# Retention's output product with three block pairs instead of two: their weight sums made ahead, the last head's norm inverted on 128x256, the head gates multiplied 1024 wide

## The chip, the cores and the metric

The kernel runs on one core of a Trainium2 chip. The metric is device time in microseconds of one execution, the median over the runs shown. The profile is that of one execution; its times count from its first instruction.

## What is computed

Two layers over 512 tokens and a model width of 1024, then a final RMSNorm, all in float32. Of each layer:

```python
h = rmsnorm(x, g_mix)
z = h @ w_in                      # attention q,k,v | retention q,k,v,g | gate_a | gate_b
A = sliding_window_sink_attention(...)
r = chunkwise_retention(rq, rk, rv)                       # 4 heads, 256 values each
r = r * lax.rsqrt(jnp.mean(r * r, axis=-1, keepdims=True) + EPS)
r = r.reshape(B, S, 1024) * jax.nn.silu(rg)
mixed = sigmoid(ga) * (A @ w_a) + sigmoid(gb) * (r @ w_b)
x = x + mixed @ w_out
x = x + jnp.square(jax.nn.relu(rmsnorm(x, g_mlp) @ w_up)) @ w_down
```

The change lies in r's norm and gate and in r @ w_b. The sizes are w_b and w_out 1024x1024, w_in 1024x5888, w_up 1024x4096.

## The kernel before, in words

**Tiles and passes.** Activations are held with features on the 128 partitions and the 512 tokens along the free axis, in eight tiles per 1024 features. Float32 products go through TensorE (PE) as float32r in three passes: each operand is split into a high half and the rest, and hi x hi, hi x lo and lo x hi are summed in PSUM (`products`, L332 to L334).

**Weight units.** All weights come in units of 128x1024 in one fixed list (`unit_order`). A unit is loaded into a raw tile (`load_until`, L196), then ScalarE (ACT) copies it to the high half (L286) and VectorE (DVE) subtracts that from the raw tile to give the low half (L287). The pool `wpool` has three buffers each for raw, hi and lo; `unit()` asks for units up to two ahead of the one that PE takes. In the rows, raw_N, hi_N and lo_N are these tiles.

**Chunks and pairs.** A plain chunk (`chunk`) makes one tile of 128 output features from one unit: 8 contraction tiles by 3 passes, 24 matmuls of 512 columns. `narrow_pair` makes two output tiles at once by Strassen's scheme: the weights and the input are cut in 2x2 blocks (tokens in halves of 256, called H), and 7 block products of 4 contraction tiles by 3 passes are done, 84 matmuls of 256 columns. It takes four units, called parts: parts 0, 1 and 2 hold two block products each, part 3 one. Some blocks are sums of weights, some inputs are sums of activations. What it needs:

- Sums of activations, made once for a product: `sum_input` for each half of it, four wide additions on lines 626, 627, 629 and 630, then splits into float32r halves (ACT L339, DVE L340). Their tiles in the rows are sums_N; the halves go to the slots r0 to r13.
- Sums of weights. Either `add_part` makes them on DVE when the part is split (L252 for part 0, L255 for part 1, L259 and L260 for part 2, into raw3_N), or, for the pairs that `PARKED` lists, `ahead()` makes them earlier in the layer: it loads both units (`raws_ahead`, L234), does four DVE additions (`sums_ahead`, L241 to L246) and stores the sums in DRAM; the parts are then loaded from there in 256 KB pieces (`load_part`, L219). Each call of `ahead()` finishes one set and starts the loads of another. Calls stand between the two chunks of qk(1), in values(0), and after units 0, 1 and 3 of w_a.

**Order of the stages in a layer.** w_in in groups and chunks with attention running as `background` steps between them; w_a; the rest of w_in, again with retention's heads as background steps; then `mixed_pair(0)` and `mixed_pair(2)` over w_b (each pair's output is multiplied by its gate on L1244 and added to the attention part on L1247), `sum_input` for the first half of w_out's input, then the four plain chunks of w_b (output multiplied on L1218 and added on L1219), `sum_input` for the second half, and w_out: two output tiles by `two_chunks` (put into x on L1288) and three pairs (c = 2, 4, 6; only the last is parked; put into x on L1296). The tiles of x are loaded back for w_out by eight loads (L1278), the gates for w_b by loads of gate_N (L1203). What comes of w_b is split into float32r halves (`split_mixed`, L339 and L340), for the pairs in steps delayed into the next pair.

**Last head.** `Head.norm` gives the inverse root mean square, on 128x512 for the last head (`inverse_rms`: ACT root, DVE reciprocal on L480). `Head.finish` multiplies each of the head's two output tiles by it (L1089), then by the gate (L1090).

**What sets the order.** The code's order, the pools and a scheduler that the framework runs when the kernel is built set the order of instructions on each engine; at run time each engine and each DMA queue goes strictly in order. All loads and stores named here are issued from SP's queue. An instruction that waits for its operands holds all behind it.

## Time and profile before

| what | before |
|---|---|
| median of 3 runs | 1468.94 us |
| lowest and highest | 1468.91 and 1469.76 us |
| span of the profiled execution | 1467.5 us, clock 1.000 |
| ACT busy | 814.6 us, 1306 instructions |
| DMA | 198.65 MB, mean 135 GB/s |

The runs give no other time for the profiled execution than its span, from the first instruction to the last; the runs' times take in what lies around it. A row of the profile reads: line, engine, operation, output from inputs by the program's names without numbers, count, busy time, mean ns of one, and the idle time ahead of it with its releaser. PE is TensorE's matmuls, PEld its weight loads.

The stages of layer 0 by the clock of this execution (length; busy time and count of PE, PEld, DVE, ACT, POOL; granted clock; DMA share; GB/s): from 285 retention's second half ends under the last chunks of w_in, from 318.7 the two w_b pairs run, from 343.3 w_b's last chunks and w_out's first two tiles, and from 368.7 the w_out pairs begin.

```profile
285.00:318.70 33.70, 33.70 (x152) 27.89 (x151) 28.27 (x35) 20.02 (x25) 0.00 (x0) 1.00 0.44 140
318.70:343.30 24.60, 24.60 (x190) 23.68 (x189) 16.26 (x22) 11.14 (x17) 0.00 (x0) 1.00 0.75 241
343.30:368.70 25.40, 25.40 (x115) 21.03 (x114) 25.14 (x34) 13.09 (x16) 0.00 (x0) 1.00 0.62 200
368.70:402.00 33.30, 33.21 (x260) 31.95 (x259) 30.16 (x46) 20.92 (x34) 0.00 (x0) 1.00 0.39 118
```

The second layer has the same stages 728 us later.

### The profile page before, as it was taken

How to read it: one execution, taken by the hardware profiler on the slowest of the kernel's cores; microseconds unless marked ns; L12 is line 12 of the kernel's file. 1: busy time of each engine (PE TensorE's matmuls, PEld its weight loads, DVE VectorE, ACT ScalarE, POOL GpSimd, SP SyncE). 2: the span in 40 equal slices, each digit the busy share in tenths (PEclk: the TensorE clock that was granted, in tenths of full speed). 3: DMA queues.
4: the chain of work that ended last, by engine and by line, in shares of the span. 5: the costliest groups of instructions: out<-in, count | busy, mean ns of one | idle time of the engine just before them, and what ended most of it. 6: DMA issues, size and time to landing. Idle time of an engine off the chain costs nothing.

```text
span 1467.5 us, 20166 instructions
## 1 busy us (share of the span) xinstructions
PE 1461.0 (100%) x7434; PEld 1246.4 (85%) x7434; DVE 1161.6 (79%) x1912; ACT 814.6 (56%) x1306; POOL 3.7 (0%) x14
## 2 busy tenths in 40 slices
PE   9999999999999999999999999999999999999998
PEld 7888888888988888888888888888989888888887
DVE  7998778678988787776678977786899877877774
ACT  7657356654684445444456653666547754455544
POOL 0000000000000000000000000000000000000000
PEclk9999999999999999999999999999999999999999
DMA  6423843356443332333543258323654432333373
GB/s 227 134 87 101 280 166 98 104 171 210 130 120 125 101 115 88 107 108 115 165 121 102 86 168 285 107 95 107 191 197 123 144 101 87 125 105 101 108 200 108
DMA packets 73346, 198.65 MB, mean 135 GB/s; under 512 B 8712, under 2 KB 8864, under 8 KB 73248
## 3 DMA queue, kind: packets, MB, share of 16 engines
q1 hardware_dynamic: 72960, 196.84, 42.5%
q8 instruction: 58, 0.95, 0.3%
q10 hardware_dynamic: 288, 0.52, 0.1%
q14 instruction: 40, 0.33, 0.1%
HBM read 173.73 MB, written 20.98 MB: 133 GB/s over the span
## 4 chain that ended last, share of the span: by engine, by line
PE 99%; DVE 0%; issue 0%; POOLq 0%; ACT 0%; DVEq 0%; ACTq 0%
PE mm L334 24%; PE mm L332 23%; PE mm L333 23%; PE mm L1356 11%; PE mm L1357 6%; PE rv L332 2%; PE rv L334 2%; PE rv L333 2%; PE score L864 1%; PE r L332 1%; PE r L334 1%; PE r L333 1%; PE pT L819 0%; PE pv L846 0%; PE pv L845 0%; PE warm L311 0%
## 5 line engine op out<-in xcount | busy, mean ns | idle before, releaser
L333 PE MATMUL mm<-r,hi 128*128 128x512 f32 (+1 forms) x1568 | 572.5, 367 | 0.0
L332 PE MATMUL mm<-r,hi 128*128 128x512 f32 (+1 forms) x1568 | 569.9, 367 | 0.0
L334 PE MATMUL mm<-r,lo 128*128 128x512 f32 (+1 forms) x1568 | 563.9, 367 | 0.2
L286 ACT ACTIVATE hi<-raw 128x1024 fp32r<-128x1024 f32 (+1 forms) x334 | 333.9, 1002 | 377.8 <-PE mm L333 206.9
L287 DVE TENSOR_TENSOR lo<-raw,hi 128x512 fp32r<-128x512 f32 (+1 forms) x335 | 384.3, 1150 | 110.8 <-ACT hi L286 109.4
L334 PEld LDWEIGHTS mm<-r,lo 128*128 128x128 f32 x1568 | 293.6, 188 | 48.8 <-DVE lo L287 1.4
L332 PEld LDWEIGHTS mm<-r,hi 128*128 128x128 f32 x1568 | 294.1, 188 | 46.5 <-ACT r L342 0.2
L333 PEld LDWEIGHTS mm<-r,hi 128*128 128x128 f32 x1568 | 294.3, 188 | 46.0
L1356 PE MATMUL mm<-r,hi 128*128 128x512 f32 x728 | 252.0, 391 | 0.0
L1357 PE MATMUL mm<-r,lo 128*128 128x256 f32 x728 | 200.3, 277 | 0.0
L1356 PEld LDWEIGHTS mm<-r,hi 128*128 128x128 f32 x728 | 136.5, 188 | 28.7 <-ACT mm L1383 0.2
L1357 PEld LDWEIGHTS mm<-r,lo 128*128 128x128 f32 x728 | 136.7, 188 | 3.2 <-DVE lo L287 0.6
L1429 ACT ACTIVATE z<-z 128x512 f32<-128x512 f32 x56 | 32.5, 624 | 51.8 <-DVE z L1409 51.8
L1436 DVE TENSOR_TENSOR x<-x,mm 128x512 f32<-128x512 f32 x56 | 37.7, 686 | 28.1 <-PE mm L334 28.1
L334 PE MATMUL rv<-hi,r 128*128 128x512 f32 x128 | 49.8, 389 | 0.0
L333 PE MATMUL rv<-lo,r 128*128 128x512 f32 x128 | 49.8, 389 | 0.0
L332 PE MATMUL rv<-hi,r 128*128 128x512 f32 x128 | 49.8, 390 | 0.0
L339 ACT ACTIVATE r<-z 128x512 fp32r<-128x512 f32 x64 | 38.5, 619 | 16.3 <-DVE z L1090 16.1
L340 DVE TENSOR_TENSOR r<-z,r 128x512 fp32r<-128x512 f32 x64 | 42.9, 685 | 4.7 <-ACT r L339 4.3
L891 ACT ACTIVATE sm<-sm,st 128x256 f32<-128x256 f32 (+1 forms) x64 | 30.1, 472 | 19.0 <-DVE st L879 18.8
L1409 DVE SCALAR_TENSOR_TENSOR z<-z,rstd 128x512 f32<-128x512 f32 x52 | 35.6, 685 | 0.6
L340 DVE TENSOR_TENSOR r<-sums,r 128x1024 fp32r<-128x1024 f32 x24 | 28.9, 1216 | 0.0
(270 smaller groups left out, 1679.2 us busy)
## 6 DMA issues: line engine op xcount, KB each, us to landing
raw<-w_in_in SPq DMA_DIRECT2D x89, 512.0 KB, 3.6
raw<-w_down_in SPq DMA_DIRECT2D x64, 512.0 KB, 3.6
raw<-w_up_in SPq DMA_DIRECT2D x32, 512.0 KB, 3.9
raw<-w_up_in SPq DMA_DIRECT2D x60, 256.0 KB, 2.9
raw<-w_a_in SPq DMA_DIRECT2D x8, 512.0 KB, 6.5
ahead<-w_b_in SPq DMA_DIRECT2D x8, 512.0 KB, 5.4
park_w_b<-ahead SPq DMA_DIRECT2D x16, 256.0 KB, 5.9
ahead<-w_up_in SPq DMA_DIRECT2D x8, 512.0 KB, 5.7
```

The costliest lines, as they stand in the source:

```text
L286: nc.scalar.activation(hi[:, at], raw[:, at], AF.Copy)
L287: last_low[:] = [nc.vector.tensor_tensor(lo[:, at], raw[:, at], f32(hi[:, at]), ALU.subtract).ins]
L332: nc.tensor.matmul(ps, ah, bh, start=start and i == 0, stop=False, **more)
L333: nc.tensor.matmul(ps, ah, bl, start=False, stop=False, **more)
L334: nc.tensor.matmul(ps, al, bh, start=False, stop=stop and i == n - 1, **more)
L339: nc.scalar.activation(hi, src, AF.Copy)
L340: nc.vector.tensor_tensor(lo, src, f32(hi), ALU.subtract)
L1356: nc.tensor.matmul(both, hi[:, c], m, start=start and k == 0, stop=False, **more)
L1357: nc.tensor.matmul(ps[:, :H], lo[:, c], m[:, 0, :], start=False, stop=k == 3 and start, **more)
L1409: nc.vector.scalar_tensor_tensor(z[:, :, at], z[:, :, at], 0.0, factor, ALU.max, ALU.mult)
L1429: nc.scalar.activation(z[:, i, :], z[:, i, :], AF.Square)
L1436: nc.vector.tensor_tensor(x[:, c, :], x[:, c, :], ps, ALU.add)
```

## The change

In each layer chunks 4 and 5 of w_b become a third `mixed_pair(4)`, and its weight sums are parked like those of the first two. `ahead()` is called once more, between the two chunks of qk(2). The last head's norm uses `inverse_rms_halved`: two roots on 64x256, a reciprocal on 128x256 (L469), and four copies that spread it to 128x512 (L472). `Head.finish` multiplies both output tiles of a head by the norm, and by the gate, in one instruction of 1024 columns each. The pairs of w_b take their PSUM banks from ps_mm only for c = 2, from ps_aux for c = 0 and 4 (before: ps_aux for 0, ps_mm for 2). The weights are packed on the host accordingly.

```diff
@@ -51,7 +51,7 @@
 ASIDE = 48
 FIRST_WIDE, LAST_WIDE = 6, 32
 BETWEEN = (0, 2, 4, 5)
-PARKED = (("w_b", 0), ("w_b", 2), ("w_out", 6), ("w_up", 4), ("w_up", 6))
+PARKED = (("w_b", 0), ("w_b", 2), ("w_b", 4), ("w_out", 6), ("w_up", 4), ("w_up", 6))
 H = T // 2
 CROSSED = (0, 1, 4, 5, 2, 3, 6, 7)
 
@@ -65,7 +65,7 @@
         return [("pair", j, part, src) for j in firsts for part in range(4)]
 
     order = plain("w_in", 26) + plain("w_a", 4) + plain("w_in", 26, 46)
-    order += pairs("w_b", 0, 2) + plain("w_b", 4, 8)
+    order += pairs("w_b", 0, 2, 4) + plain("w_b", 6, 8)
     order += plain("w_out", 2) + pairs("w_out", 2, 4, 6)
     for what, q, i in mlp_sequence():
         if what == "first":
@@ -1080,16 +1080,16 @@
 
             def norm(self):
                 self.inv = temp("inv")
-                (inverse_rms if self.h == 3 else inverse_rms_apart)(self.parts, RET_V, self.inv)
+                (inverse_rms_halved if self.h == 3 else inverse_rms_apart)(self.parts, RET_V, self.inv)
 
             def finish(self):
                 h = self.h
+                two = rg_tiles[h]
+                nc.vector.tensor_tensor(two, two, self.inv.unsqueeze(1).broadcast_to([P, 2, T]), ALU.mult)
+                nc.vector.tensor_tensor(two, self.both, two, ALU.mult)
                 for e in range(2):
-                    z = rg.pop(2 * h + e)
-                    nc.vector.tensor_tensor(z, z, self.inv, ALU.mult)
-                    nc.vector.tensor_tensor(z, self.rr[e], z, ALU.mult)
                     hi, lo = slots.one(), slots.one()
-                    split(view(hi), view(lo), z)
+                    split(view(hi), view(lo), rg.pop(2 * h + e))
                     ret[2 * h + e] = (hi, lo)
 
         def retention(pair):
@@ -1173,7 +1173,7 @@
             slots.give(*t[1])
 
         background.append(retention(0))
-        qk(2)
+        qk(2, between=ahead)
         qk(3)
         values(1)
         drain()
@@ -1243,7 +1243,7 @@
             def put(i, at, src, z):
                 return nc.vector.tensor_tensor(two[:, i, at], two[:, i, at], src, ALU.mult)
 
-            narrow_pair(ps_aux if c == 0 else ps_mm, delayed_step(), form_of(by_form_r), block_r, put)
+            narrow_pair(ps_mm if c == 2 else ps_aux, delayed_step(), form_of(by_form_r), block_r, put)
             nc.vector.tensor_tensor(two, two, x[:, own : own + 2, :], ALU.add)
             delayed.extend(partial(split_mixed, c + i, gates[c + i]) for i in range(2))
 
@@ -1251,7 +1251,7 @@
             at = slice(tokens * H, tokens * H + H)
             return [tuple(m[:, at] for m in rT[CROSSED[k]]) for k in range(4 * half, 4 * half + 4)]
 
-        for c in (0, 2):
+        for c in (0, 2, 4):
             mixed_pair(c)
         all_of(delayed)
         delayed.clear()
@@ -1260,7 +1260,7 @@
         homes_m = [forms_home(), None, forms_home(), None]
         by_form_m = [h and h[1] for h in homes_m]
         sum_input(by_form_m, gate_tiles[:2], 0)
-        for c in range(4, KD):
+        for c in range(6, KD):
             if c % 2 == 0:
                 gate_tile()
             chunk("w_b", layer, rT, put_mixed(c))
@@ -1559,8 +1559,8 @@
 
 def _ret_units(w):
     cols = _crossed(np.arange(D))
-    paired = _units_chunks(w[cols], cols[:T])
-    return [_swapped(u) if i % 2 else u for i, u in enumerate(paired)] + _units_chunks(w, cols[T:])
+    paired = _units_chunks(w[cols], cols[: 6 * P])
+    return [_swapped(u) if i % 2 else u for i, u in enumerate(paired)] + _units_chunks(w, cols[6 * P :])
 
 
 def _up_units(w):
```

DVE, last head of retention, layer 0, before (z_2514 holds the head's two gates, rr_2496 its outputs, inv_2628 the norm, lo_2758 and lo_2793 are weight units, sums_2695 is `sum_input`'s):

```order
L340 TENSOR_TENSOR r11_87<-z_2349,r11_87 128x512
L287 TENSOR_TENSOR lo_2758<-raw_2668,hi_2757 128x1024
L480 RECIPROCAL inv_2628<-inv_2628 128x512
L287 TENSOR_TENSOR lo_2793<-raw_2720,hi_2792 128x1024
L1089 TENSOR_TENSOR z_2514<-z_2514,inv_2628 128x512 x2
L1090 TENSOR_TENSOR z_2514<-rr_2496,z_2514 128x512 x2
L627 TENSOR_TENSOR sums_2695<-z_2514,sums_2695 128x512
```

The same place after (z_2524, rr_2506, own_2641 with inv_2638, lo_2770 and lo_2805, sums_2707):

```order
L287 TENSOR_TENSOR lo_2770<-raw_2682,hi_2769 128x1024
L469 RECIPROCAL own_2641<-own_2641 128x256
L287 TENSOR_TENSOR lo_2805<-raw_2732,hi_2804 128x1024
L1088 TENSOR_TENSOR z_2524<-z_2524,inv_2638 128x1024
L1089 TENSOR_TENSOR z_2524<-rr_2506,z_2524 128x1024
L627 TENSOR_TENSOR sums_2707<-z_2524,sums_2707 128x512
```

The reciprocal has half the columns and stands between the same two weight splits; four multiplications of 512 have become two of 1024.

DVE, from the last w_b pair's end, before (gate_3020 is the second pair's output, gate_3162 and gate_3234 are those of the plain chunks, mm_N their PSUM banks):

```order
L287 TENSOR_TENSOR lo_3167<-raw_3093,hi_3166 128x1024
L627 TENSOR_TENSOR sums_3152<-gate_3020,sums_3152 128x512
L629 TENSOR_TENSOR sums_3153<-gate_3020,gate_2893 128x512
L287 TENSOR_TENSOR lo_3202<-raw_3127,hi_3201 128x1024
L340 TENSOR_TENSOR r1_77<-gate_3020,r1_77 128x512 x2
L630 TENSOR_TENSOR sums_3153<-gate_3020,sums_3152 128x512
L340 TENSOR_TENSOR r7_83<-sums_3152,r7_83 128x4x256
L1218 TENSOR_TENSOR gate_3162<-mm_3170,gate_3162 128x512
L1218 TENSOR_TENSOR gate_3162<-mm_3205,gate_3162 128x512
L287 TENSOR_TENSOR lo_3241<-raw_3164,hi_3240 128x1024
```

After, from the same point of the third pair (gate_3163 is its output, gate_3032 and gate_2905 are those of the first two, gate_3305 that of the two chunks left, lo_3273 the split of chunk 7's unit, lo_3312 and lo_3347 those of w_out's first two units):

```order
L287 TENSOR_TENSOR lo_3273<-raw_3202,hi_3272 128x1024
L627 TENSOR_TENSOR sums_3295<-gate_3032,sums_3295 128x512
L630 TENSOR_TENSOR sums_3296<-gate_3032,sums_3295 128x512
L340 TENSOR_TENSOR r7_83<-sums_3295,r7_83 128x4x256
L1244 TENSOR_TENSOR gate_3163<-gate_3163,mm_3165 128x256
L1218 TENSOR_TENSOR gate_3305<-mm_3315,gate_3305 128x512
L340 TENSOR_TENSOR r10_86<-sums_3296,r10_86 128x4x256
L1247 TENSOR_TENSOR gate_3163<-gate_3163,x_75 128x1024
L287 TENSOR_TENSOR lo_3312<-raw_3236,hi_3311 128x1024
L1219 TENSOR_TENSOR gate_3305<-gate_3305,x_75 128x512
L287 TENSOR_TENSOR lo_3347<-raw_3270,hi_3346 128x1024
```

Before, the splits of two chunks (lo_3167, lo_3202) and `sum_input`'s additions lie between the last pair and the split of w_out's first unit (lo_3241). Now chunk 7's split and the second half of those additions stand ahead of the last pair's L1247, and w_out's first unit (lo_3312) right behind it.

DVE, from the third part of w_out's first pair (lo_3401 before, lo_3472 after) to the next pair's first split (lo_3468 before, lo_3539 after); L343 and L429 prepare the MLP's input, L678 and L675 are additions of the pair that read PSUM:

```order
L287 TENSOR_TENSOR lo_3401<-raw3_3397,hi_3400 128x1024
L255 TENSOR_TENSOR raw2_3430<-raw_3393 128x512
L287 TENSOR_TENSOR lo_3433<-raw_3238,hi_3432 128x512
L1296 TENSOR_TENSOR x_75<-x_75,mm_3389 128x256
L343 SCALAR_TENSOR_TENSOR r8_84<-x_75,r8_84 128x512
L678 TENSOR_TENSOR z_3392<-mm_3390,eu_3391 128x256
L287 TENSOR_TENSOR lo_3468<-raw_3393,hi_3467 128x1024
L675 TENSOR_TENSOR z_3392<-mm_3388,eu_3391 128x256
```

```order
L287 TENSOR_TENSOR lo_3472<-raw3_3468,hi_3471 128x1024
L1296 TENSOR_TENSOR x_75<-x_75,mm_3460 128x256
L255 TENSOR_TENSOR raw2_3501<-raw_3464 128x512
L287 TENSOR_TENSOR lo_3504<-raw_3309,hi_3503 128x512
L287 TENSOR_TENSOR lo_3539<-raw_3464,hi_3538 128x1024
L343 SCALAR_TENSOR_TENSOR r8_84<-x_75,r8_84 128x512
L678 TENSOR_TENSOR z_3463<-mm_3461,eu_3462 128x256
L675 TENSOR_TENSOR z_3463<-mm_3459,eu_3462 128x256
```

The split of the next pair's first part stands ahead of L678 now, and behind it before; L675 is behind both in either order.

SP's queue, the loads for w_out and those among them, before (raw_3164, raw_3199: the first two units; raw_3236, raw2_3273, raw_3238: pieces of the first pair):

```order
L196 DMA raw_3164<-w_out_in 128x1024
L1278 DMA x_75<-xT_in 128x512
L1203 DMA gate_3162<-aside_91 128x1024
L1203 DMA gate_3234<-aside_91 128x1024
L196 DMA raw_3199<-w_out_in 128x1024
L228 DMA raw2_3273<-w_out_in 128x512
L1278 DMA x_75<-xT_in 128x512
L223 DMA raw_3236<-w_out_in 128x512
L225 DMA raw_3238<-w_out_in 128x1024
```

After (raw_3202: chunk 7's unit; raw_3236, raw_3270: w_out's first two; raw_3307, raw2_3344, raw_3309: pieces of the first pair):

```order
L196 DMA raw_3202<-w_b_in 128x1024
L196 DMA raw_3236<-w_out_in 128x1024
L196 DMA raw_3270<-w_out_in 128x1024
L1203 DMA gate_3305<-aside_91 128x1024
L228 DMA raw2_3344<-w_out_in 128x512
L223 DMA raw_3307<-w_out_in 128x512
L1278 DMA x_75<-xT_in 128x512 x2
L225 DMA raw_3309<-w_out_in 128x1024
```

The load of the pair's second unit (raw_3309, which L252 reads) stands right behind two loads of x now; before, one load of x and a piece of 256 KB stood there.

## The prediction

> **What bounds the kernel now.** I read the page first: busy time and the chain that ended last.
>
> ```profile
> PE 1461.0 (100%) x7434; PEld 1246.4 (85%) x7434; DVE 1161.6 (79%) x1912; ACT 814.6 (56%) x1306; POOL 3.7 (0%) x14
> PE 99%; DVE 0%; issue 0%; POOLq 0%; ACT 0%; DVEq 0%; ACTq 0%
> ```
>
> TensorE (PE) is the chain: 99% of it. So a change is worth what it takes out of PE's own matmul time, less what it makes PE wait. Next I looked at who makes PE wait at all (the chain of waits, TensorE's rows for weight splits).
>
> ```profile
> PEld mm L334 <- DVE lo L287: 1.4, 6, 0.3
> PEld mm L1357 <- DVE lo L287: 0.6, 2, 0.3
> ```
>
> Eight waits, 2.0 us in 1467.5, all for the low half of a weight unit, which VectorE (DVE) makes on line 287. Last, the stretches around the change in layer 0 (columns: length; busy time and count of PE, PEld, DVE, ACT, POOL; granted clock; DMA share; GB/s). The w_b pairs begin at 318.7, w_b chunk 4 at 336.8, and the first w_out pair has PE to itself from 372.4.
>
> ```profile
> 150.00:200.00 50.00, 50.00 (x227) 41.63 (x226) 40.63 (x61) 18.41 (x26) 0.00 (x0) 1.00 0.85 279
> 200.00:285.00 85.00, 85.00 (x407) 72.01 (x406) 61.54 (x104) 54.08 (x86) 0.00 (x0) 1.00 0.28 87
> 318.70:336.80 18.10, 18.10 (x155) 18.10 (x154) 12.81 (x17) 10.08 (x16) 0.00 (x0) 1.00 0.78 250
> 343.30:372.40 29.10, 29.10 (x136) 24.30 (x135) 28.84 (x39) 13.78 (x17) 0.00 (x0) 1.00 0.57 187
> 376.00:400.00 24.00, 23.91 (x201) 23.50 (x200) 20.96 (x32) 16.35 (x27) 0.00 (x0) 1.00 0.47 139
> ```
>
> PE is full in each, at full clock. But DVE has 0.3 us free in the 29.1 us from 343.3, where the weights of w_b's chunks and of w_out are split: there a little more DVE work, or a little less PE time to hide it in, can reach PE. That is where the change works.
>
> **The change, part by part.**
>
> *PE.* Per layer the third pair takes away two chunks (2 x 8 x 3 = 48 matmuls 512 wide) and puts 7 products of 4 blocks by 3 passes = 84 matmuls 256 wide. In the windows below PE does only the one kind and then only the other.
>
> ```profile
> 319.00:336.80 17.80, 17.80 (x153) 1.00 0.78 250
> 344.00:368.60 24.60, 24.60 (x110) 1.00 0.62 199
> ```
>
> The counts take in one or two that only reach into a window; without them one narrow matmul starts each 17.8/151 = 0.118 us and a wide one each 24.6/108.5 = 0.227. So 48 x 0.227 = 10.90 against 84 x 0.118 = 9.91: 0.98 us per layer, 1.97 for two. [...]
>
> *Sums made ahead.* One more set per layer: two loads of 512 KB, four DVE additions, four stores of 256 KB, and the pair's weights are read in pieces of 256 KB.
>
> ```profile
> L241 DVE TENSOR_TENSOR ahead<-ahead 128x512 f32<-128x512 f32 x10 | 6.8, 685 | 0.0
> ahead<-w_b_in SPq DMA_DIRECT2D x8, 512.0 KB, 5.4
> park_w_b<-ahead SPq DMA_DIRECT2D x16, 256.0 KB, 5.9
> ```
>
> DVE: 4 x 0.685 = 2.7 us, beside 9.4 us that it has free in 150 to 200 and 23.5 in 200 to 285. DMA: 2.1 MB, at 279 GB/s 7.5 us, where the engines are 85% busy. The call moved into qk(2) carries the last set's sums and stores past the first loads of that stage on SP's queue, and holds a load for one store's 5.9 us. Behind it stand weight units, which are split up to two units ahead of PE (2 x 24 matmuls of 0.227 = 10.9 us); the cover is that lead and the 28% DMA share of the next 85 us. I cost it at nothing. Without the cover some of the 7.5 us shows; bounds 0 and +1 per layer, since the late bytes are spread over several units.
>
> *Last head's norm, gates.* The reciprocal shrinks, two ACT pieces and four copies come.
>
> ```profile
> L480 DVE RECIPROCAL inv<-inv 128x512 f32<-128x512 f32 x2 | 6.7, 3355 | 3.2 <-ACT inv L479 3.2
> L469 DVE RECIPROCAL own<-own 128x256 f32<-128x256 f32 x2 | 3.5, 1752 | 5.9 <-ACT own L468 5.9
> L472 ACT ACTIVATE rstd<-own 64x256 f32<-64x256 f32 x8 | 3.3, 416 | 0.8 <-DVE own L469 0.7
> ```
>
> DVE gets 3.36 - 1.75 = 1.6 us, ACT pays 4 x 0.42 = 1.7 in front of the multiplication, so its result is not earlier. All of it ends by 318, and PE waits for nothing there (no row of the waits): 0, between -0.1 and +0.3 per layer (the 0.3 of the longest wait above).
>
> *The queue on DVE.* This is the term that I cannot read off. DVE's order now has no slack chunks between the third pair and w_out. I follow it by starts, since DVE's instructions overlap at their ends.
>
> ```profile
> 361.52 0.68 DVE L255 TENSOR_TENSOR raw<-raw 128x512 f32<-128x512 f32 x1
> 362.12 1.21 DVE L287 TENSOR_TENSOR lo<-raw,hi 128x1024 fp32r<-128x1024 f32 x1
> 363.25 0.68 DVE L340 TENSOR_TENSOR r<-gate,r 128x512 fp32r<-128x512 f32 x1
> ```
>
> A 512-wide one takes 0.60 of the queue, a 1024-wide one 1.14, not their 0.68 and 1.22. On before's clock PE starts the third pair at 336.8 and ends its third part at 346.7 (9.9 later); DVE's addition on L675 follows at 347.0, and, after it (0.36) and four 512-wide ones, chunk 7's split (lo_3273) at 349.8. From that split to the split of the third part of w_out's first pair (lo_3472) stand 11 of 1024, 21 of 512 and one of 256 (0.36): 12.5 + 12.6 + 0.4 = 25.5, so it is ready at 375.4. PE begins that part 36 narrow matmuls (half of the first part, all of the second) after 372.4 - 1.0 = 371.4, at 375.7, and takes the low half with its third matmul, 375.9. That is 0.5 us of slack, where before it was about 2:
>
> ```profile
> 373.57 1.23 DVE L287 TENSOR_TENSOR lo<-raw,hi 128x1024 fp32r<-128x1024 f32 x1
> 376.92 0.28 PE L334 MATMUL mm<-r,lo 128*128 128x256 f32 x1
> ```
>
> Two waits can eat it. The low half of r7_83 needs the sum of L627 and then an ACT copy of 1.05 us (L339), with one 512-wide instruction to cover it: up to 0.6. And L252 needs a 512 KB load (raw_3309) that now stands behind two loads of x on SP's queue.
>
> ```profile
> raw<-w_out_in SPq DMA_DIRECT2D x8, 512.0 KB, 3.8
> x<-xT_in SPq DMA_DIRECT2D x15, 256.0 KB, 5.7
> L339 ACT ACTIVATE r<-sums 128x1024 fp32r<-128x1024 f32 x24 | 24.9, 1053 | 3.0 <-DVE sums L627 1.6 <-DVE sums L630 1.5
> ```
>
> That load is issued when the split of w_out's first unit (lo_3312) is over, 358.4 by the same count with the first wait in it, and lands 3.8 to 5.7 later, 362.2 to 364.1; DVE comes to L252 at 363.1. So 0 to 1.0 us. The third part's split ends between 375.4 and 377.0.
>
> One stall goes. Before, the next pair's first split stood behind an addition (L678) that waits for PE:
>
> ```profile
> 378.30 0.42 DVE L678 TENSOR_TENSOR z<-mm,eu 128x256 f32<-128x256 f32 x1 [0.33 <-PE mm L334]
> 378.64 1.22 DVE L287 TENSOR_TENSOR lo<-raw,hi 128x1024 fp32r<-128x1024 f32 x1
> ...
> 379.63 0.28 PE L333 MATMUL mm<-r,hi 128*128 128x256 f32 x1
> ...
> 379.91 0.39 PE L334 MATMUL mm<-r,lo 128*128 128x256 f32 x1
> ...
> 380.13 0.28 PE L332 MATMUL mm<-r,hi 128*128 128x256 f32 x1
> ```
>
> PE's starts are 0.28 and 0.22 apart instead of 0.12: 0.27 lost. Now that split stands ahead of L678, so the 0.27 is won, if DVE comes to it in time. What is late next is the second part of that pair:
>
> ```profile
> 380.10 0.74 DVE L343 SCALAR_TENSOR_TENSOR r<-x,r 128x512 fp32r<-128x512 f32 x1
> 380.76 0.68 DVE L429 TENSOR_TENSOR acc<-acc,sq 128x512 f32<-128x512 f32 x1
> 382.57 1.22 DVE L287 TENSOR_TENSOR lo<-raw,hi 128x1024 fp32r<-128x1024 f32 x1
> 384.49 0.28 PE L334 MATMUL mm<-r,lo 128*128 128x256 f32 x1
> ```
>
> Before, PE took it at 384.49. In the new order its split ends 7.7 us behind the third part's (five of 512, three of 256, two of 1024 and two fused ones of 0.66 between starts, the last counted to its end): at 383.1 to 384.7. PE would want it at 384.49 - 0.98 - 0.27 = 383.24. So the gain per layer at this point is 1.25 in the best case and -0.2 in the worst of these. I take the split of the third part at 376.2, in the middle, hence 383.9 and a gain of 0.6 per layer. A later stall, 0.36 at the third w_out pair, keeps its order (L675 ahead of the split) and stays.
>
> [...]
>
> *Sum.* The execution shown spans 1467.5; the median of the runs, 1468.94, lies 1.4 above for what is around the span. 1467.5 - 2 x 0.6 = 1466.3 in the span, 1467.7 in the time; both layers have the same rows.
>
> **The rivals.**
>
> - *DVE is in time everywhere.* Both waits are hidden: gain 1.25 x 2 = 2.5, time 1466.4; with the 0.36 stalls gone too, 1465.7. For it: ACT is half idle, and such loads land in 3.8. Against it: DVE's 0.3 us free in 29.
> - *DVE gives it all back.* Both waits count in full: -0.2 per layer, time 1469.3, no change. For it: the loads of x stand in front.
> - *Slower.* The load for L252 comes later still. From 364.1 on each microsecond costs PE one, in both layers; to lose more than 0.2% (2.9 us, about what a measurement of this kernel can tell from no change) it must land at 365.4, 7.0 after its issue: time 1471.8. For it is the row below, weights loaded while the DMA engines were 85% busy; against it, that from 343 to 372 they are 57% busy.
>
> ```profile
> raw<-w_a_in SPq DMA_DIRECT2D x8, 512.0 KB, 6.5
> 339.78 1.23 DVE L287 TENSOR_TENSOR lo<-raw,hi 128x1024 fp32r<-128x1024 f32 x1 [0.53 <-ACT hi L286]
> L332 PEld LDWEIGHTS mm<-r,hi 128*128 128x128 f32 x1568 | 294.1, 188 | 46.5 <-ACT r L342 0.2
> ```
>
> - *The pair's weights are too late.* The third pair's second part stands in the queues where chunk 5 stood, whose split ended at 341.0 (second row); PE comes to it at 336.8 + 36 x 0.118 = 341.1 and takes its low half some four matmuls on, 341.5. Each microsecond later than 0.5 is lost: 1 us over it turns 1467.7 into 1469.7.
> - *Full durations count.* If the DVE queue moved by 0.68 and 1.22, the two stretches would be longer by 2.6 and 0.9: 3.5 later than my middle case, -2.9 per layer, 1474.7. If narrow matmuls went at the pace of their weight loads (third row), 84 x 0.188 = 15.8 for 10.9, 1478.7. [...]
>
> **How the numbers follow.** The middle case has 0.45 (1466.9 to 1468.5 alone), DVE in time 0.22, all given back 0.17, late pair weights 0.08, slower 0.06, full durations 0.02. Faster by over 0.2% (below 1466.0) needs the other stalls gone: 0.06 of DVE in time and 0.02 of the middle case, 0.08. Slower (above 1471.9): 0.06 + 0.02 + 0.01 of the late weights, 0.09. The rest, 0.83, is within 0.2%. The range 1466.1 to 1470.2 reaches from the full gain to the late weights; the 0.17 at its two ends stay out.
>
> **What would show it.** Right: 72 more matmuls, 96 fewer of 512 and 168 more of 256; two starts of 0.12 where 379.63 had 0.28; DVE without gaps from the third pair's end to 376, and PE's waits for L287 moved to the third or second part of a w_out pair, 0.3 to 0.9 us per layer. Wrong: the windows between 150 and 285 with PE not full; narrow matmuls more than 0.118 apart; a wait for L287 inside the w_b pairs; a wait of L252 for its load of over 1 us, or none and no PE wait at all.

## The result, and the profile after

| | before | changed |
|---|---|---|
| median of 20 runs | 1468.93 us | 1471.44 us |
| lowest and highest | 1468.51, 1470.16 | 1468.48, 1472.30 |
| span of the profiled execution | 1467.5 us | 1470.2 us |

The ratio is 1.0013 (ratios here and below are of means, here 1471.00 and 1469.11 us), with a 95% interval of 1.0007 to 1.0019: slower by 0.07 to 0.19%. The medians alone give 1.0017. Predicted were 1467.7 us and a range from 1466.1 to 1470.2. The changed kernel's runs also spread over 3.8 us, those of before over 1.7.

The page of the changed kernel, busy time and the chain that ended last:

```profile
PE 1461.3 (99%) x7506; PEld 1248.8 (85%) x7506; DVE 1165.7 (79%) x1912; ACT 821.7 (56%) x1326; POOL 3.7 (0%) x14
PE 97%; DVE 1%; DMA 1%; issue 0%; ACT 0%; SPq 0%; POOLq 0%; DVEq 0%; ACTq 0%
```

TensorE is no longer 99% of the chain. DVE and DMA have a per cent each: stretches in which TensorE's next step hung on them. Who makes TensorE wait (the chain of waits, its weight loads):

```profile
PEld mm L334 <- DVE lo L287: 4.0, 11, 1.0
PEld mm L332 <- ACT eu L665: 1.1, 2, 0.5
PEld mm L1357 <- DVE lo L287: 0.6, 2, 0.3
```

The first row was 1.4 us in six waits; the second is new. TensorE's starts in layer 0, at the third part of w_out's first pair, show two of these waits in one place:

```profile
376.26 0.28 PE L334 MATMUL mm<-r,lo 128*128 128x256 f32 x1
376.88 0.39 PE L332 MATMUL mm<-r,hi 128*128 128x256 f32 x1 [0.34 <-ACT eu L665]
377.11 0.28 PE L333 MATMUL mm<-r,hi 128*128 128x256 f32 x1
377.75 0.39 PE L334 MATMUL mm<-r,lo 128*128 128x256 f32 x1 [0.37 <-DVE lo L287]
```

Starts 0.62, 0.23 and 0.64 apart where they should be 0.12: with the slow one behind the last, 1.24 us lost. In layer 1 there is a stretch that has no counterpart in layer 0 of this execution, in w_b's third pair and the chunk behind it (first TensorE, then ACT, whose high halves wait for a load):

```profile
1069.98 0.28 PE L333 MATMUL mm<-r,hi 128*128 128x256 f32 x1
1070.48 0.38 PE L334 MATMUL mm<-r,lo 128*128 128x256 f32 x1 [0.22 <-DVE lo L287]
...
1076.50 0.40 PE L333 MATMUL mm<-r,hi 128*128 128x512 f32 x1
1077.43 0.51 PE L334 MATMUL mm<-r,lo 128*128 128x512 f32 x1 [0.53 <-DVE lo L287]
```

```profile
1068.11 1.06 ACT L286 ACTIVATE hi<-raw 128x1024 fp32r<-128x1024 f32 x1 [4.36 <-DMA raw<-w_b_in]
1075.05 1.06 ACT L286 ACTIVATE hi<-raw 128x1024 fp32r<-128x1024 f32 x1 [1.58 <-DMA raw<-w_b_in]
```

The next table adds up what TensorE loses in each place, in us: each step from one start to the next less 0.118 (256 columns) or 0.227 (512), counted where more than 0.095 is left. The last column is another execution of the changed kernel, the run `after_again` below:

| place | before | changed | again |
|---|---|---|---|
| w_b's third pair and chunk behind it, layer 0 / layer 1 | 0 / 0 | 0 / 1.78 | 1.04 / 0 |
| w_out's first pair, layer 0 / layer 1 | 0 / 0 | 1.24 / 1.09 | 1.48 / 1.51 |
| w_out's second pair, each layer | 0.27 | 0.30 | 0.30 |

For the profiled execution: 1.78 + 1.24 + 1.09 + 2 x 0.03 = 4.2 lost, 1.97 won by fewer columns, so 2.2 longer. The first attention matmul starts at 51.35 instead of 50.67, 0.7 more: at the very start of an execution the steps between matmuls of 512 columns are mostly 0.43 instead of 0.227, and there are 14 such long steps here and 11 before. Together 2.9; the span is 2.7 longer. That start varies from run to run (50.27 in the other execution of the changed kernel), so I do not count it as an effect of the change.

What the change does by itself is as worked out. In the same 17.8 us the narrow matmuls come at the same rate, and TensorE is full between 150 and 285 with one more set of sums:

```profile
319.00:336.80 17.80, 17.80 (x152) 17.76 (x151) 12.12 (x16) 10.08 (x16) 0.00 (x0) 1.00 0.80 262
150.00:200.00 50.00, 50.00 (x227) 41.64 (x226) 39.61 (x58) 17.43 (x24) 0.00 (x0) 1.00 0.87 287
200.00:285.00 85.00, 85.00 (x404) 71.80 (x403) 63.84 (x104) 53.73 (x87) 0.00 (x0) 1.00 0.33 108
L241 DVE TENSOR_TENSOR ahead<-ahead 128x512 f32<-128x512 f32 x12 | 8.2, 685 | 0.0
L469 DVE RECIPROCAL own<-own 128x256 f32<-128x256 f32 x4 | 7.0, 1753 | 9.3 <-ACT own L468 9.3
```

### The profile page after: what moved, and what is told of

Its sections match the earlier page's. It is cut to its first block, busy times and chain, and to the rows that moved or that the text cites. A ratio compares the mean times of both kernels' runs of the same rounds, so it can differ in the third digit from the quotient of the medians.

```text
span 1470.2 us, 20388 instructions
## 1 busy us (share of the span) xinstructions
PE 1461.3 (99%) x7506; PEld 1248.8 (85%) x7506; DVE 1165.7 (79%) x1912; ACT 821.7 (56%) x1326; POOL 3.7 (0%) x14
## 4 chain that ended last, share of the span: by engine, by line
PE 97%; DVE 1%; DMA 1%; issue 0%; ACT 0%; SPq 0%; POOLq 0%; DVEq 0%; ACTq 0%
PE mm L334 23%; PE mm L332 23%; PE mm L333 23%; PE mm L1356 11%; PE mm L1357 6%; PE rv L334 2%; PE rv L333 2%; PE rv L332 2%; PE score L864 1%; DMA raw<-w_b_in 1%; PE r L332 1%; PE r L334 1%; PE r L333 1%; DVE lo L287 1%; PE pT L819 0%; PE pv L846 0%
## 5 line engine op out<-in xcount | busy, mean ns | idle before, releaser
L287 DVE TENSOR_TENSOR lo<-raw,hi 128x1024 fp32r<-128x1024 f32 (+1 forms) x339 | 387.7, 1147 | 115.4 <-ACT hi L286 113.9
L332 PEld LDWEIGHTS mm<-r,hi 128*128 128x128 f32 x1592 | 298.6, 188 | 46.9 <-ACT eu L665 1.1
L333 PEld LDWEIGHTS mm<-r,hi 128*128 128x128 f32 x1592 | 299.2, 188 | 44.9
L1356 PEld LDWEIGHTS mm<-r,hi 128*128 128x128 f32 x728 | 136.5, 188 | 28.7 <-ACT mm L1383 0.2
L340 DVE TENSOR_TENSOR r<-z,r 128x512 fp32r<-128x512 f32 x64 | 42.4, 684 | 5.0 <-ACT r L339 4.6
L339 ACT ACTIVATE r<-z 128x512 fp32r<-128x512 f32 x64 | 37.9, 620 | 11.2 <-DVE z L1089 11.2
L339 ACT ACTIVATE r<-s 128x512 fp32r<-128x512 f32 (+3 forms) x32 | 14.1, 465 | 29.7 <-DVE s L1042 16.6
```

The source lines that it names most:

```text
L287: last_low[:] = [nc.vector.tensor_tensor(lo[:, at], raw[:, at], f32(hi[:, at]), ALU.subtract).ins]
L332: nc.tensor.matmul(ps, ah, bh, start=start and i == 0, stop=False, **more)
L333: nc.tensor.matmul(ps, ah, bl, start=False, stop=False, **more)
L339: nc.scalar.activation(hi, src, AF.Copy)
L340: nc.vector.tensor_tensor(lo, src, f32(hi), ALU.subtract)
L1356: nc.tensor.matmul(both, hi[:, c], m, start=start and k == 0, stop=False, **more)
```

## The experiments

Each time stands beside the kernel before, run on the same chip with it.

**The parts of the change.** `third_only` undoes the edits to norm and gates, `norm_gates` makes these alone in the kernel before:

```diff
-                (inverse_rms_halved if self.h == 3 else inverse_rms_apart)(self.parts, RET_V, self.inv)
+                (inverse_rms if self.h == 3 else inverse_rms_apart)(self.parts, RET_V, self.inv)
...
-                two = rg_tiles[h]
-                nc.vector.tensor_tensor(two, two, self.inv.unsqueeze(1).broadcast_to([P, 2, T]), ALU.mult)
-                nc.vector.tensor_tensor(two, self.both, two, ALU.mult)
+                # for each e: z * inv, rr[e] * z, 512 wide, as before the change
```

> The third pair and its sums made ahead alone; the last head's norm and the gate multiplications as before the change. Theory A, the loss is the third pair's: its weights come late in one layer (1.8 us of stalls) and the third part of w_out's first pair is split late in both (1.24 us each): 1471.4, within 0.7 of the changed kernel, with PE waits for L287 of 4 us in all. Theory B, the small edits to norm and gates cost it: 1467 to 1468, and PE waits of under 2 us.

> The kernel before with the small edits alone: norm on 128x256, gates 1024 wide, no third pair. Theory A: 1468.9, within 0.4 of before, the same eight waits for L287 of 2.0 us. Theory B: 1470.5 to 1471.5.

Third pair alone: 1471.70 (before 1469.19), ratio 1.0016 (1.0007 to 1.0025). Norm and gates alone: 1469.28, ratio 1.0000 (0.9991 to 1.0008), and the same waits as before. The loss is the third pair's; the small edits cost and bring nothing measurable. In the profile of the third pair alone the w_b pairs wait in neither layer; w_out's first pair loses 1.6 and 1.5 us at the places known from the changed kernel, and in layer 1 another 0.9 at its first part.

**Later loads of x.** `x_late` takes the loads of x out from among the third pair's loads. Only SP's order changes.

```diff
-                    queue.dma_start(raws[i][:, at], weights[name][layer, j][:, at])
+                    loads[i] = queue.dma_start(raws[i][:, at], weights[name][layer, j][:, at]).ins
...
         for c in range(KD):
-            nc.sync.dma_start(x[:, c, :], source[:, c, :])
+            with tc.issue_after(loads[state["next"] + 1]):
+                nc.sync.dma_start(x[:, c, :], source[:, c, :])
```

> The changed kernel with the eight loads of x queued behind the load of w_out's second unit; no other engine's order changes. Theory A1, the third pair's weights are late because two loads of x (256 KB each) stand among them: the waits for L287 inside the w_b pairs go (1.8 us in layer 1), the late third part in w_out stays at 1.24 us per layer: 1469.6 (1469.0 to 1470.3). Theory A2, the pieces of the parked pair alone are too much for the time: 1471.4, with the waits of layer 1 still there. Should x come late for w_out: a new wait of L1288 for its load.

1469.02 against 1469.19, ratio 0.9999 (0.9991 to 1.0008): 2.4 below the changed kernel's median. The sequences of TensorE, DVE and ACT are the same as in the changed kernel, instruction by instruction. The profiled span is 1466.3, 1.2 below before's. The loads of the third pair in the changed kernel, layer 1 from 1055 to 1066 (DMA issues, KB each, median us from issue to landing), and the same part of x_late:

```profile
raw<-w_b_in SPq DMA_DIRECT2D x4, 256.0 KB, 6.2
x<-spill SPq DMA_DIRECT2D x2, 256.0 KB, 4.0
```

```profile
raw<-w_b_in SPq DMA_DIRECT2D x3, 256.0 KB, 4.1
```

Two loads of x, 0.5 MB, stood in front of the pair's pieces; without them a piece lands in 4.1 instead of 6.2. No wait of TensorE for L287 is left in the w_b pairs. More than A1 expected came back, because the stall in w_out shrank too. Why, DVE's timeline in layer 0 shows, first of the changed kernel, then of x_late (the splits of chunk 6, of chunk 7, of the third part):

```profile
346.56 1.23 DVE L287 TENSOR_TENSOR lo<-raw,hi 128x1024 fp32r<-128x1024 f32 x1 [0.76 <-ACT hi L286]
...
351.45 1.22 DVE L287 TENSOR_TENSOR lo<-raw,hi 128x1024 fp32r<-128x1024 f32 x1 [0.60 <-ACT hi L286]
...
376.49 1.21 DVE L287 TENSOR_TENSOR lo<-raw,hi 128x1024 fp32r<-128x1024 f32 x1
```

```profile
345.01 1.23 DVE L287 TENSOR_TENSOR lo<-raw,hi 128x1024 fp32r<-128x1024 f32 x1 [0.24 <-ACT hi L286]
...
349.55 1.22 DVE L287 TENSOR_TENSOR lo<-raw,hi 128x1024 fp32r<-128x1024 f32 x1
...
374.78 1.22 DVE L287 TENSOR_TENSOR lo<-raw,hi 128x1024 fp32r<-128x1024 f32 x1
```

In layer 0 of the changed kernel TensorE did not wait in the w_b pairs, but DVE did: its split of chunk 6 waited 0.76 for a high half that was late with its load,

```profile
345.46 1.06 ACT L286 ACTIVATE hi<-raw 128x1024 fp32r<-128x1024 f32 x1 [0.88 <-DMA raw<-w_b_in]
```

and what stood behind it on DVE went with it (the addition right behind, L678, began at 347.70, in x_late at 346.15). Chunk 7's split then waited 0.60 for its own high half. That one too was late with its load, which stood behind two more loads of x. The rows are from SP's queue, the list of issues and ACT; the last is the same copy in x_late:

```profile
343.16 0.82 SPq L1278 DMA_DIRECT2D x<-xT_in  x2
344.29 0.33 SPq L196 DMA_DIRECT2D raw<-w_b_in  x1
raw<-w_b_in SPq DMA_DIRECT2D x1, 512.0 KB, 6.0
350.35 1.06 ACT L286 ACTIVATE hi<-raw 128x1024 fp32r<-128x1024 f32 x1 [3.83 <-DVE sums L629]
```

```profile
346.90 1.06 ACT L286 ACTIVATE hi<-raw 128x1024 fp32r<-128x1024 f32 x1 [1.93 <-DMA raw<-w_b_in]
```

The load was issued at 344.29 and landed 6.0 later, at 350.3; ACT began at 350.35. The row names L629, which happened to end at the same moment; the copy does not need it, for in x_late it begins 1.45 before L629 (348.35). Chunk 7's split starts 1.9 later than in x_late, 1.1 of it beside the first attention matmul (51.35 against 50.54). From there to the third part's split it is 25.0 and 25.2 us; DVE waits in between for no more than 0.5 and 0.6 us in all, so it has no idle time from which to make it up. So a load that no row of TensorE's waits shows in layer 0 was paid for 30 us later.

`before_x_late` makes the same edit in the kernel before. There the scheduler also moved three of DVE's instructions by a place or two in each layer (L1218, L1219, L340).

> The kernel before with x queued behind the load of w_out's second unit. Theory: x among the loads costs only where three parked pairs follow one another, so nothing changes here: 1469.2 (1468.7 to 1469.7). Rival, x costs wherever it stands: 1467.5 or less, and the gain of x later in the changed kernel says nothing about the third pair.

1469.07 against 1469.25, ratio 1.0000 (0.9991 to 1.0009): nothing, as expected. Of these two kernels, x among the loads costs only the one with three pairs.

**The same kernel again.** `after_again` is the changed kernel unaltered.

> The changed kernel once more, for a second profile. Theory, the third pair's weights come late by chance of the transfers, w_out's first pair by DVE's order: the stall of 1.1 to 1.3 us at the first w_out pair shows in both layers again, stalls in the w_b pairs in none, one or both layers and of other sizes. Rival, they are tied to layer 1 (whose x comes from a DRAM tile that the kernel wrote): again layer 1 alone, 1.8 us.

1470.58 in one run. The stall at w_out's first pair is there in both layers, 1.48 and 1.51, more than the 1.1 to 1.3 expected; the late weights are in layer 0 this time, 0.35 in the pair and 0.37 at the chunk (1.04 with the slow starts behind them), none in layer 1 (table above). They are not tied to a layer, and in the changed kernel's first profile they go with the landing: a piece from w_b took 6.2 us in the layer where TensorE waited in the pair and 5.2 in the other; in third_only, where it did not wait there, 5.3 in both. Whether this is why the runs spread is not shown: those of x_late, whose profile has no late weights, spread as much (1468.06 to 1471.54).

**The third pair's sums made in place.** `unparked` takes ("w_b", 4) out of PARKED and the call out of qk(2).

> The changed kernel with the third pair's sums made in place (L252 to L260): 0.75 MB less is loaded in the stretch of the pair and no call in qk(2), for four additions of 0.60 more on DVE there, where it has idle time. Theory A1, x among the loads is what is too much: late weights partly stay, and the additions come on top: 1471.5 to 1473. Theory A2, the parked pieces are too much: the waits in the w_b pairs go: 1469.5 to 1470.5, w_out's first pair still late.

1479.21 against 1469.49, ratio 1.0067 (1.0055 to 1.0078). Worse than either theory. TensorE's longest waits are these, the first for an addition on DVE that reads PSUM; what held that addition up is not shown:

```profile
PEld mm L332 <- DVE z L675: 5.3, 2, 3.1
PEld mm L334 <- DVE lo L287: 4.2, 7, 1.8
```

So it tells nothing on x; it shows that in this order of DVE the pair needs its sums ahead.

**Less on DVE's queue.** Five runs. `out_parked` makes the sums of w_out's first pair ahead (a seventh set, called in qk(3)); `no_add` leaves out L1219, so that the attention part is missing from the last two chunks' output; `pool_third` puts L259 and L260 on POOL for w_out's pairs; `x_late_pool` and `x_late_pe_pool` (with the matmuls' order below) do so with x later.

```diff
+            engine = nc.gpsimd if order[i][4] == "w_out" else nc.vector
-            nc.vector.tensor_tensor(raws[i][:, LEFT], w1[:, LEFT], w2[:, RIGHT], ALU.subtract)
-            nc.vector.tensor_tensor(raws[i][:, RIGHT], z2[:, RIGHT], z2[:, LEFT], ALU.subtract)
+            engine.tensor_tensor(raws[i][:, LEFT], w1[:, LEFT], w2[:, RIGHT], ALU.subtract)
+            engine.tensor_tensor(raws[i][:, RIGHT], z2[:, RIGHT], z2[:, LEFT], ALU.subtract)
```

> The changed kernel with the weight sums of w_out's first pair made ahead too (a seventh set, its call in qk(3)). That takes four additions of 0.60 us between starts, 2.4 us, out of DVE's queue ahead of the split of that pair's third part. Theory A: the split was 1.1 us late, so the stall of 1.24 us per layer goes and the late pair weights stay: 1469.0 (1468.3 to 1469.8). Rival, the third part is late for its load or for ACT's queue: 1471.4 and PE still waits at the third part. Rival, the seventh set costs loads: 1472 or more, with waits between 150 and 285 us.

> The changed kernel without the addition on L1219 (the attention part is left out of the last two chunks' output): two instructions of 512, 1.2 us, less on DVE's queue between 355 and 366 us of each layer; loads unchanged. Theory, a full DVE queue makes the third part of w_out's first pair late: its split comes 1.2 us sooner, the wait for L287 there goes and the wait for ACT's copy on L665 (0.6 with its follow-up) stays: 1470.2 (1469.5 to 1470.9). Rival, the split waits for something else (its load, its high half): 1471.4.

> The changed kernel with the two additions that make the third part's sums of w_out's pairs (L259, L260) on POOL, which is idle: 1.2 us less on DVE's queue ahead of the split of the third part, nothing left out, loads unchanged. Theory, DVE's full queue makes that part late: the wait for L287 there goes (0.64 of the 1.24 us per layer), the wait for L665 (0.6) and the late pair weights stay: 1470.2 (1469.4 to 1471.0). Rival, the lateness comes from somewhere else: 1471.4. No run so far shows such an addition on POOL; should one take over 4 us, the third part is later: 1473 or more.

> Both: x queued behind the load of w_out's second unit, and L259, L260 on POOL. With x later DVE was already in time for the third part, so the additions' 1.2 us free only the next pair (0.1 to 0.3 per layer) and the copy on L665 a little: 1468.6 (1467.8 to 1469.2), against 1469.0 for x later alone.

> All three: x later, the matmuls of w_out's first pair in the code's order, L259 and L260 on POOL. With the first two TensorE waited for the sums' split on L340 (1.0 us in layer 0) and 0.63 at the next pair in each layer, both behind DVE's queue; 1.2 us less there takes them: 1467.2 (1466.7 to 1468.2), faster than the kernel before. Rival, DVE is not the bound there: 1468.5 as without POOL.

| run | time | before beside it | ratio, 95% |
|---|---|---|---|
| out_parked | 1491.54 | 1469.19 | 1.0150 (1.0136 to 1.0164) |
| no_add | 1481.47 | 1469.49 | 1.0082 (1.0069 to 1.0095) |
| pool_third | 1482.63 | 1469.25 | 1.0091 (1.0077 to 1.0105) |
| x_late_pool | 1480.67 | 1469.25 | 1.0090 (1.0075 to 1.0104) |
| x_late_pe_pool | 1480.86 | 1469.25 | 1.0083 (1.0069 to 1.0096) |

All missed. Each edit made the scheduler order the work anew, also far from its place. In no_add the second w_out pair loses 1.98 us and two places in w_up 1.76 and 0.79, in each layer, and the same 1.76 (a wait for ACT's root) and 0.78 stand in the three POOL runs. That is not all of it: in pool_third TensorE also loses 4.3 and 6.4 us at w_out in the two layers, where the additions were moved, against 1.9 and 1.7 in the changed kernel. The waits of no_add:

```profile
PEld mm L334 <- DVE lo L287: 7.5, 8, 2.0
PEld mm L332 <- ACT own L468: 3.6, 2, 1.8
```

out_parked has no stall at the third part of w_out's first pair, but 2.2 and 2.3 us in the two layers where retention's scores wait for DVE, with the seventh set now in its queue, and 3.6 to 4.8 us from the last part of that pair to the first of the next. As tests of the queue's length all five are inconclusive. The POOL runs show one thing besides, told at the end.

**The order of matmuls and two exchanges on DVE.** In w_out's first pair the scheduler had put the last products of the first part behind the second part's, so that only 5 matmuls stood between the end of one accumulation and its next use, and ACT's copy on L665 (0.37 us) had to fit between. `after_pe` restores the code's order there; `x_late_pe` does so with x later. Around the second pair the scheduler then also ordered DVE and ACT anew.

```diff
-            multiply(e, part, False, form(0))
+            first_done = multiply(e, part, False, form(0))
...
-            multiply(b, part, True, form(1), False)
+            with tc.issue_after(first_done) if apart else ExitStack():
+                multiply(b, part, True, form(1), False)
...                                                        # the same for multiply(a, part, False, block(1, 0), False)
```

> The changed kernel with TensorE's matmuls of w_out's first pair in the code's order: the products of its second part behind those of its first, so that ACT's copy on L665 has 24 matmuls of cover, not 5. Theory 1, DVE alone sets the time there: the wait for L665 goes and the waits for DVE (L340, then L287) take its place: 1471.4, within 0.5. Theory 2, the matmuls' order costs 0.6 us per layer by itself: 1470.2.

> x later, as before, and the matmuls of w_out's first pair in the code's order. With x later DVE was in time for the third part, and the wait for L665, 0.6 per layer, was what was left. Theory: it goes too, less up to 0.3 per layer where TensorE now waits for the sums' split on L340: 1468.0 (1467.6 to 1468.8). Rival, something else takes its place: 1469.0.

after_pe: 1471.40 against 1469.49, ratio 1.0014 (1.0005 to 1.0022). The wait for L665 is gone, and a wait for the sums' split took its place, as theory 1 has it:

```profile
372.95 0.28 PE L332 MATMUL mm<-r,hi 128*128 128x256 f32 x1
373.90 0.38 PE L333 MATMUL mm<-r,hi 128*128 128x256 f32 x1 [0.67 <-DVE r L341]
```

x_late_pe: 1468.52 against 1469.49, ratio 0.9994 (0.9985 to 1.0003); in layer 0 TensorE waits 0.87 for the same split (1.14 lost with the slow start behind it), in layer 1 not at all.

`after_pe_swap` and `x_late_pe_swap` put that split ahead of the split of the second part (lines 340 and 287); these two instructions change places and nothing else on DVE. `x_late_pe_swap2` also puts the next pair's L255 behind the split of its first part.

```diff
+                with tc.issue_after(hold[i]) if i in hold else ExitStack():     # hold: the sums' split on L340
                     last_low[:] = [nc.vector.tensor_tensor(lo[:, at], raw[:, at], f32(hi[:, at]), ALU.subtract).ins]
...
+            with tc.issue_after(last_low[0]) if order[i][2:] == (4, 1, "w_out") else ExitStack():    # swap2 alone
                 nc.vector.tensor_tensor(raws[i][:, LEFT], w1[:, RIGHT], w1[:, LEFT], ALU.subtract)
```

> The changed kernel, the matmuls of w_out's first pair in the code's order and, on DVE, the sums' split (L340) ahead of the split of that pair's second part instead of behind it: same work, two instructions exchanged. Theory, the wait for L340 goes but the third part's split is where it was, behind the same work: its wait for L287 grows to about 1.1 us per layer, the time stays: 1471.4 (1470.8 to 1472). Rival, the exchange frees it: 1470.0.

> x later, the matmuls in the code's order, and the exchange on DVE. With x later the third part is in time within 0.2 us, so the exchange takes the wait for L340 (1.0 us in layer 0 of the last profile, none in layer 1) and brings no more than 0.2 of another: 1468.0 (1467.5 to 1468.5). Rival, the wait moves to the third part in full: 1468.5.

> That, and the next pair's addition on L255 behind the split of its first part instead of ahead of it (0.60 us sooner for the split that TensorE waited 0.63 for in each layer): 1467.0 (1466.5 to 1467.8), faster than the kernel before. Rival, the addition is then late for the pair's second part and the wait only moves on: 1468.0.

after_pe_swap: 1471.72 against 1469.30, ratio 1.0015 (1.0006 to 1.0024). The wait for L340 went and the one for the third part's L287 is back, 0.57 and 1.1 in the two layers with the slow start behind it (here line 288), with another 0.8 in layer 1 at the pair's first part:

```profile
376.15 0.28 PE L334 MATMUL mm<-r,hi 128*128 128x256 f32 x1
376.73 0.38 PE L335 MATMUL mm<-r,lo 128*128 128x256 f32 x1 [0.30 <-DVE lo L288]
```

Three orders of the same work, one time: from the first attention matmul on, the profiled executions of the changed kernel, after_pe and after_pe_swap take 1418.9, 1418.8 and 1418.8. The losses only stand elsewhere: the second pair, for one, loses 0.74 per layer in both other orders instead of 0.30. In the changed kernel DVE sets the end there, and only the name and place of the wait change. With x later the same exchange left none at the first pair:

| run (x later, and) | profiled span | first w_out pair, layers 0 / 1 | second pair | time, before 1469.2 to 1469.5 |
|---|---|---|---|---|
| nothing more | 1466.3 | 0.71 / 0.61 | 0 / 0.25 | 1469.02 |
| matmuls in the code's order | 1467.4 | 1.24 / 0.11 | 0.74 / 0.74 | 1468.52 |
| that and the split exchanged | 1467.1 | 0 / 0 | 0.66 / 0.74 | 1469.03 |
| that and L255 later | 1465.7 | 0.32 / 0.23 | 0.50 / 0.40 | 1469.04 |

Each edit did in the trace what it should at its own place (the last also moved one PSUM addition). The last one leaves 1.5 us lost at the two pairs in both layers together, where nothing but x later leaves 1.6 and the changed kernel 2.9, and the span of its profile is 1.8 below before's (1.4 beside the first attention matmul). In the times none of the four is told from before: x_late_pe_swap 0.9998 (0.9989 to 1.0007), x_late_pe_swap2 0.9997 (0.9988 to 1.0006); against the 1468.0 and 1467.0 expected, these two missed by 1.0 and 2.0. Their runs still spread, x_late's from 1468.06 to 1471.54, and the profiled executions of x_late (1468.08) and x_late_pe_swap2 (1467.53) lie at the low end, so they are not typical. What the other executions wait for was not profiled.

## Why the prediction was wrong, by its own steps

- **Matmuls.** Right: 72 more in all, and 0.118 and 0.227 between starts, 0.52 of the time for half the columns. The 0.98 per layer was won and spent.
- **Sums made ahead; norm and gates.** Rightly put at nothing: TensorE full from 150 to 285, L241 now twelve times 0.685, the reciprocal 1.75 for 3.36, and norm_gates at 1.0000.
- **The queue on DVE.** The count held: from the start of chunk 7's split to the ready low half of the third part 25.5 were counted without waits and 26.2 measured (351.45 to 377.70), with 0.40 of the first feared wait (L340 for L339, of up to 0.6) and 0.09 of the second (L252 for its load, of up to 1.0). What failed is the start of that count, "chunk 7's split (lo_3273) at 349.8". It was 351.45, on before's clock 350.8, because two high halves waited for loads (0.76 and 0.60 on DVE). x_late, where they came in time, has it at 349.55, and there the third part's split ends at 376.0, against the 376.2 that I took. I had followed the loads of x only in front of L252's load, where they cost 0.09; the two in front of the pair's pieces and the two in front of chunk 7's unit I put at nothing. So the split of the third part ended at the upper end of what I had given (377.0 on before's clock), and with it the term "gain 0.6 per layer" became a loss of 0.1 to 0.6: 0.98 against 1.24 and 1.09 here, 1.48 and 1.51 in the other execution.
- **The pair's weights are too late.** I gave this rival 0.08. It occurred in both executions of the changed kernel that were profiled, each time in one layer; in that of third_only it did not. The step that failed is where its slack came from: the split of chunk 5, which had only two pairs' loads in front of it, and a 0.5 us margin on it. With a third pair's pieces, and x among them, a piece from w_b took 5.2 and 6.2 us to land in the two layers; with the same pieces and x later, 4.1 in layer 1.
- **The sum.** The two rivals, late weights and a late DVE, stood as alternatives with a price each, 1469.7 and 1469.3. In these runs they had one cause: a load that was late behind x delayed DVE's splits, whether or not TensorE waited for one of them first. Chunk 7's split waited 0.60 and 0.53 in the two layers, though in the second TensorE had already lost 1.78. Both prices were paid together. The gain of 0.6 per layer was a loss of 0.29 and 0.14 in the one execution, 0.53 and 0.55 in the other (0.98 less the first pair's loss and 0.03), which makes 1.6 and 2.3 us; late weights of 1.78 and 1.04 came on top. 1467.7 becomes 1471.1 and 1471.0; the median is 1471.4. The 1.4 from span to time was too small as well: in the runs of either kernel that give both it is 1.7 to 1.9.
- **What I did not look at.** TensorE's own order in w_out's first pair. It is a real wait, 0.6 to 0.7 per layer in x_late, and hidden under DVE's in the changed kernel: in after_pe it is gone and the time is the same.
- The stall of 0.27 that was to go went from the second pair's first part and came back as 0.30 at its second, the one named as late next.

That the loads of x among those of w_b cause the loss is shown (x_late, with before_x_late beside it), and that in w_out's first pair the lateness of DVE decides, not the order of matmuls, is shown by three orders with one time. That a shorter DVE queue would give the gain is not shown, since the tries changed too much else. The two profiled executions are 2.0 and 1.7 longer than before's from the first attention matmul on; the means differ by 1.9, the medians by 2.5. Why x later gives back the loss and not also the gain of 1.2 is open: its one profiled execution is 1.1 shorter than before's from the first attention matmul on, its median 0.2 lower.

## What to carry to other kernels

When a faster form of a product changes which weights are read and when, look first at the loads: here the third pair reads seven pieces of 256 KB in 9.9 us, where the two chunks read the bytes of four in 10.9, and two loads of x among them were paid for: a piece landed in 6.2 us instead of 4.1, and the median was 2.4 us longer. A load that is late for an engine off the critical path need not show in the bound engine's waits where it happens: in layer 0 two of DVE's splits waited 0.76 and 0.60 us for high halves that were late with their loads, DVE waited no more than 0.5 us in the 25 that followed, and TensorE's wait came 30 us on. So do not price two rivals as alternatives before asking whether one of them causes the other, and when an experiment must keep the order of all else, exchange two instructions rather than leave one out.

## What the runs showed of the hardware

Additions on DVE took longer beside an addition on POOL. The timelines of pool_third, POOL and then DVE:

```profile
365.18 1.45 POOL L260 TENSOR_TENSOR raw<-raw 128x512 f32<-128x512 f32 x1 [362.55 <-DMA raw<-w_out_in]
367.87 1.67 POOL L261 TENSOR_TENSOR raw<-raw 128x512 f32<-128x512 f32 x1 [1.23 <-DVE raw L255]
```

```profile
365.39 1.79 DVE L1220 TENSOR_TENSOR gate<-gate,x 128x512 f32<-128x512 f32 x1
...
368.31 1.78 DVE L630 TENSOR_TENSOR sums<-gate 128x512 f32<-128x512 f32 x1
```

DVE's rows of this size take 0.68 otherwise; the two that began beside a POOL addition took 1.79 and 1.78 and ended 0.55 behind it. Moving 2 x 0.60 us off DVE cost it 2 x 1.1. In x_late_pool it is the same: the additions at 363.66 and 366.58, beside POOL's of 363.46 and 366.13, took 1.79 and 1.78. Why is not shown.

The start of an execution varies by itself: the first attention matmul starts at 51.35 and 50.27 us in two executions of the changed kernel, and at 50.67 and 50.54 in those of before and x_late, with the edits elsewhere. That difference of 1.1 us is about the difference that most of these runs were to tell apart.
